# The homes of the tiles that TensorE reads: all at multiples of 512 bytes of a partition

## The chip, the cores and the metric

The kernel runs on one core of a Trainium2 chip. Its time is the device time of one execution in microseconds (us), the median of several runs. Engines are called by the profile's names: PE is TensorE's matmul, PEld its weight load, DVE is VectorE, ACT is ScalarE, POOL is GpSimd, SP is SyncE, which issues most DMAs. A tile's home is the byte of each SBUF partition at which it begins.

## What is computed

A two-layer encoder trunk on two sequences, 512 and 256 tokens, with width 1024; all in fp32:

```python
for i in range(DEPTH):                       # 2 layers
    h = rms_norm(x, norm_mix[i])
    if i % N_MIXERS == 0:                    # layer 0: attention in a window of +-128
        x = x + window_attention(h, ...)
    else:                                    # layer 1: gated depthwise convolution of width 3
        x = x + short_conv(h, ...)
    h = rms_norm(x, norm_mlp[i])
    x = x + jnp.square(jax.nn.relu(h @ mlp_w_up[i])) @ mlp_w_down[i]     # 1024 -> 4096 -> 1024
    gate = jax.nn.sigmoid(rms_norm(x, norm_ple[i]) @ ple_w_gate[i])
    x = x + (p[i] @ ple_w_proj[i]) * gate
return rms_norm(x, final_norm)
```

## The kernel before

The 768 tokens of both sequences lie along the free dimension, the 1024 features in eight blocks of 128 partitions. A product is a set of matmuls of 128 x 128 weights with 512, 384 or 256 moving columns (`H` = 384 is half of the tokens).

fp32 precision comes from three fp32r matmuls: weights and activations are each split in a high part (ScalarE copies it to fp32r) and a low part (VectorE subtracts), and high x high, high x low and low x high are added in PSUM. Weights arrive by DMA in `wraw` and are split to `whi` and `wlo`, to `zhi` and `zlo`, or to `vhi` and `vlo`. The MLPs and the convolution use a fast scheme for 2 x 2 blocks with seven products (`product7`, L498 in the profile's rows); it needs sums of weight blocks, in the tiles `sum`, and sums of activation blocks, the `t` tiles. `group` (L145) and `group2` (L135) are the plain products. Each matmul loads its own weights. The full-precision fp32 matmuls of the last norm are at L1884.

The order of the instructions on ScalarE, TensorE and VectorE is written out by hand (`manual_schedule`); semaphore waits follow from the tiles. That order and those waits are not touched by the change.

SBUF is handed out in pools, each pool's tiles one behind the other in the order in which a tag is first asked for. Tiles begin at multiples of 32 bytes. The pools that matter here:

- `const`: `vec` (gains of the norms), `sink`, `ident`, `ones32`, `ones`, `eps`.
- `slots`: the slots S0 to S31 of 768 fp32 columns (3072 bytes), in which nearly all activations live (`xs`, `t`, `act`, `aos`, `ys`, `gw`). A few tiles there have 769 columns, which the allocator rounds up to 3104 bytes (S8, S9).
- `wp`: `whi`, `wlo` (two each) and `wraw` (three), 4096 bytes each.
- `attn` and `tmpA`: what the attention stage needs, among it `ph`, `pl` and `vv` (its probabilities and values) and `L`.
- `more` and `tmpB`: take the same room after the attention stage: `zhi`, `zlo`, `vhi`, `vlo`, `sum`, slots S32 to S41 (S40 and S41 with 769 columns) and temporaries.

The small tiles of `const` shift all that stands behind them, so that few homes are at multiples of 512.

```python
def slot(i, name, dt=F32R, n=T):
    return (slots if i < 32 else more).tile([P, n], dt, tag=f"S{i}", name=name)
```

Of the kernel before, what the change touches and what calls it, by code (L numbers as in the profile page):

```python
# [11 lines left out]
F32 = mybir.dt.float32  # L12
# [6 lines left out]
P = 128  # L19
# [3 lines left out]
T = sum(SEQS)  # L23
# [5 lines left out]
CH = 1024  # L29
# [19 lines left out]
def trunk_kernel(ctx: ExitStack, tc: tile.TileContext, a: dict, out: bass.AP):  # L49
# [3 lines left out]
    const = ctx.enter_context(tc.tile_pool(name="const", bufs=1))  # L53
    main = ctx.enter_context(tc.tile_pool(name="main", bufs=1))
    slots = ctx.enter_context(tc.tile_pool(name="slots", bufs=1))
    wp = ctx.enter_context(tc.tile_pool(name="wp", bufs=2))
# [4 lines left out]
    act.preload_act_table_set(EXP_LN)  # L61
    tmp, turn, shift = None, 0, 2


    vec = const.tile([P, 7 * KB + 3 * KB], F32, name="vec")
    def gain(i, m):
# [6 lines left out]
    ident = const.tile([P, P], F32, name="ident")  # L73
# [4 lines left out]
    ones32 = const.tile([P, P], F32, name="ones32")  # L78
    dve.memset(ones32[:], 1.0)
    ones = const.tile([P, P], F32R, name="ones")  # L80
    dve.tensor_copy(ones[:], ones32[:])
    eps = const.tile([P, 1], F32, name="eps")
    dve.memset(eps[:], EPS)


    def split(hi, lo, src):
# [60 lines left out]
    more = None  # L147

    def slot(i, name, dt=F32R, n=T):

        return (slots if i < 32 else more).tile([P, n], dt, tag=f"S{i}", name=name)
# [20 lines left out]
    class Norm:  # L172


        n = T
# [327 lines left out]
    def mixer_attention():  # L503
        s1, s2 = ExitStack(), ExitStack()
        psum = s2.enter_context(tc.tile_pool(name="psK", bufs=3, space=PSUM))
        nonlocal tmp
        ap = s1.enter_context(tc.tile_pool(name="attn", bufs=2))
        tmp = s1.enter_context(tc.tile_pool(name="tmpA", bufs=3))


# [45 lines left out]
        with tc.manual_schedule(engines=order):  # L556
# [34 lines left out]
            for k in range(2):  # L591
                ph, pl = slot(10 + k, "p0h"), slot(12 + k, "p0l")
# [26 lines left out]
        with s1:  # L619
# [54 lines left out]
            vv = ap.tile([P, T // P, KV, 2, HD], F32R, name="vv", bufs=1)  # L674
# [202 lines left out]
        return xa, aos  # L877

    xa, aos = mixer_attention()
    psum = ctx.enter_context(tc.tile_pool(name="ps", bufs=8, space=PSUM))  # L880
    more = ctx.enter_context(tc.tile_pool(name="more", bufs=1))
    tmp = ctx.enter_context(tc.tile_pool(name="tmpB", bufs=1))
    pairs = [main.tile([P, 2, T], F32, tag=f"x{j}", name="x") for j in range(KB // 2)]

    def x(m, o=0, n=T):
# [1337 lines left out]
```

## Time and profile before

| | |
|---|---|
| time, median of 3 runs | 1649.18 us (1648.55 to 1649.38) |
| the profiled execution: its span, first to last instruction | 1647.0 us |
| PE busy | 1630.8 us, 9375 matmuls |
| PEld busy | 1576.5 us |
| DVE busy | 1406.5 us |
| ACT busy | 979.6 us |
| DMA | 166.35 MB, mean 101 GB/s |

For the profiled execution the page gives the span alone; the median of the runs stands 2.2 us above it. The profile's matmuls are pipelined: one starts while the one before it is still draining, so that PE's busy time says when PE had work and not how fast it ran. How fast it ran is read from the starts: the time of a stretch without a gap, divided by its matmuls. A row's "mean ns of one" holds this interval and a tail that does not depend on the shape.

### The profile page before, as it was taken

What the parts mean: (1) busy time and instruction counts of PE and PEld (TensorE: products, weight loads), DVE (VectorE), ACT (ScalarE), POOL (GpSimd) and SP (SyncE); (2) the same over time, 40 slices, a digit from 0 to 9 for tenths busy, and PEclk for the clock granted to TensorE, in tenths of its full rate; (3) what the DMA queues carried; (4) which work ended last, traced back from release to release, by engine and by line L of the source; (5) the groups of instructions that cost most, each with busy time, mean ns of one, the idle gap of its engine ahead of it and who ended that gap; (6) DMA issues with size and microseconds to landing.
All of it is one profiled execution on the core that took longest, in us unless ns stands there. A gap on an engine that the chain in (4) does not pass through costs nothing.

```text
span 1647.0 us, 24367 instructions
## 1 busy us (share of the span) xinstructions
PE 1630.8 (99%) x9375; PEld 1576.5 (96%) x9375; DVE 1406.5 (85%) x2289; ACT 979.6 (59%) x1566; POOL 82.5 (5%) x116
## 2 busy tenths in 40 slices
PE   9999999999999999999999999999999999999997
PEld 7988889999999999999999999999999999999986
DVE  7599898899889889889888777778889888988996
ACT  7378766866556556557763443555555555655764
POOL 0211000000000000000000000000000000000000
PEclk9999999999999999999999999999999999999999
DMA  8754412443323333235512122112333323333332
GB/s 272 205 134 129 141 46 84 125 106 96 90 76 91 97 96 92 72 93 147 144 64 81 66 77 77 64 64 69 92 97 96 89 76 93 96 97 92 96 117 99
DMA packets 57460, 166.35 MB, mean 101 GB/s; under 512 B 7248, under 2 KB 10832, under 8 KB 57344
## 3 DMA queue, kind: packets, MB, share of 16 engines
q1 hardware_dynamic: 45440, 139.89, 26.3%
q0 software_dynamic: 11904, 24.91, 8.6%
q8 instruction: 73, 1.20, 0.3%
q14 instruction: 43, 0.35, 0.1%
HBM read 143.02 MB, written 10.48 MB: 93 GB/s over the span
## 4 chain that ended last, share of the span: by engine, by line
PE 88%; DVE 8%; ACT 3%; issue 1%; DMA 0%; DVEq 0%; SPq 0%; ACTq 0%
PE a L498 34%; PE mm L145 9%; PE b L498 8%; PE mm L135 5%; PE d L498 5%; PE c L498 5%; PE B L498 4%; PE C L498 4%; PE gate L145 2%; PE gate L1621 2%; PE gate L1596 2%; PE pt L786 1%; PE p L1115 1%; PE p L1218 1%; PE O L796 1%
## 5 line engine op out<-in xcount | busy, mean ns | idle before, releaser
L448 ACT ACTIVATE vhi<-wraw 128x512 fp32r<-128x512 f32 x71 | 44.7, 630 | 134.6 <-PE B L498 90.3
L498 PE MATMUL a<-xs,whi 128*128 128x384 f32 x624 | 121.6, 336 | 0.0
L1391 DVE TENSOR_TENSOR x<-x,a 128x384 f32<-128x384 f32 x128 | 70.3, 553 | 55.5 <-PE a L498 55.3
L498 PE MATMUL a<-t,zhi 128*128 128x384 f32 x568 | 116.2, 337 | 0.0
L498 PE MATMUL a<-t,whi 128*128 128x384 f32 x568 | 115.8, 336 | 0.0
L498 PE MATMUL a<-act,whi 128*128 128x384 f32 x512 | 110.3, 337 | 0.0
L498 PEld LDWEIGHTS a<-xs,whi 128*128 128x128 f32 x624 | 109.9, 188 | 0.2 <-DVE y L1325 0.2
L498 PE MATMUL b<-t,zhi 128*128 128x384 f32 x536 | 108.8, 336 | 0.5 <-DVE v L261 0.5
L498 PEld LDWEIGHTS a<-t,zhi 128*128 128x128 f32 x568 | 100.5, 188 | 0.4 <-DVE t L368 0.4
L498 PEld LDWEIGHTS a<-t,whi 128*128 128x128 f32 x568 | 100.4, 188 | 0.4 <-ACT d L1493 0.4
L476 DVE TENSOR_TENSOR wlo<-wraw,whi 128x1024 fp32r<-128x1024 f32 x74 | 90.1, 1218 | 8.0 <-ACT whi L448 8.0
L498 PEld LDWEIGHTS b<-t,zhi 128*128 128x128 f32 x536 | 94.7, 188 | 0.8 <-DVE v L261 0.8
L476 DVE TENSOR_TENSOR wlo<-sum,whi 128x1024 fp32r<-128x1024 f32 x71 | 86.7, 1221 | 6.7 <-ACT whi L448 6.7
L498 PEld LDWEIGHTS a<-act,whi 128*128 128x128 f32 x512 | 91.3, 188 | 0.0
L448 ACT ACTIVATE whi<-sum 128x1024 fp32r<-128x1024 f32 x71 | 74.8, 1053 | 27.1 <-PE a L498 22.7
L448 ACT ACTIVATE whi<-wraw 128x1024 fp32r<-128x1024 f32 x76 | 79.9, 1051 | 7.0 <-PE C L498 7.0
L476 DVE TENSOR_TENSOR zlo<-sum,zhi 128x1024 fp32r<-128x1024 f32 x69 | 84.0, 1217 | 0.0
L448 ACT ACTIVATE zhi<-sum 128x1024 fp32r<-128x1024 f32 x71 | 75.1, 1058 | 12.1 <-DVE sum L424 11.2
L145 PE MATMUL mm<-xs_mix,whi 128*128 128x512 f32 (+1 forms) x320 | 81.0, 341 | 0.0
L1081 ACT ACTIVATE y<-y 128x768 f32<-128x768 f32 x62 | 52.0, 839 | 44.7 <-DVE y L1078 44.7
L362 ACT ACTIVATE t<-y 128x768 fp32r<-128x768 f32 x64 | 52.5, 840 | 43.4 <-DVE y L353 42.1
L498 PE MATMUL a<-xs,wlo 128*128 128x384 f32 x312 | 67.2, 337 | 0.0
(388 smaller groups left out, 4496.1 us busy)
## 6 DMA issues: line engine op xcount, KB each, us to landing
wraw<-in_up SPq DMA_DIRECT2D x64, 512.0 KB, 3.6
wraw<-in_down SPq DMA_DIRECT2D x64, 512.0 KB, 4.3
wraw<-in_w_in SPq DMA_DIRECT2D x24, 512.0 KB, 3.4
vlo<-in_down POOLq DMA_DIRECT2D x32, 256.0 KB, 5.8
wraw<-in_gate SPq DMA_DIRECT2D x16, 512.0 KB, 4.2
vlo<-in_up POOLq DMA_DIRECT2D x28, 256.0 KB, 5.6
pj<-pjs SPq DMA_DIRECT2D x16, 384.0 KB, 2.9
wraw<-in_w_q SPq DMA_DIRECT2D x8, 512.0 KB, 4.7
```

What stands on the lines that cost most here:

```text
L135: pe.matmul(t, lhsT=w, rhs=x[:, o:e], start=first and i == 0 and j == 0, stop=last and i == n - 1 and j == 2)
L145: pe.matmul(ps[:, o:e], lhsT=w, rhs=x[:, o:e], start=n == 0, stop=n == len(order) - 1)
L362: act.activation(t[0][:], (self.q1, self.q2)[i][:], AF.Copy)
L448: act.activation(hi[:], src, AF.Copy)
L476: dve.tensor_tensor(lo[:], src, hi[:].bitcast(F32), ALU.subtract)
L498: pe.matmul(ps, lhsT=a, rhs=b, start=start and i == 0, stop=i == len(terms) - 1, skip_group_check=True)
L786: pe.transpose(pt[:, h * P : (h + 1) * P], lg[h // 2][:, h % 2, b * P : (b + 1) * P], ident[:],)
L796: pe.matmul(O[:], lhsT=v, rhs=ph[:], start=b == 0, stop=False)
L1081: act.activation(t[:], t[:], AF.Square)
L1391: dve.tensor_tensor(t[:, o : o + H], t[:, o : o + H], f, op)
L1596: pe.matmul(t, lhsT=w[wi][k], rhs=norm.xs[part][k][:, o:e], start=k == order[0] and wi == part == 0, stop=k == order[-1] and wi == 1,)
L1621: pe.matmul(t, lhsT=wt, rhs=xt[:, b:e], start=i == j == 0 and xt is xh, stop=i == len(ts) - 1 and j == 1,)
```

## The change

The change asks for tiles earlier and in another order, so that they get other homes, and never uses what it asked for in that place: `homes` takes a tile of a tag from its pool, which fixes the tag's home, and the later code gets the same tag at that home. Fillers ("before", 96 columns, and so on) push the first of them to a multiple of 512. Tiles of odd size (`vec`, `sink`, `eps`, the 769-column slots, the bias and statistics tiles of attention) come last in their pools.

```diff
+    WIDE = 8, 9, 40, 41
+
+    def homes(pool, *tags):
+        for tag, n, *bufs in tags:
+            bufs = bufs[0] if bufs else 1
+            for _ in range(bufs):
+                pool.tile([P, n], F32, tag=tag, name="home", bufs=bufs)
+
+    def slot_homes(pool, some):
+        homes(pool, *[(f"S{i}", T) for wide in (False, True) for i in some if (i in WIDE) == wide])
+
+    homes(const, ("before", 96), ("ident", P), ("ones32", P), ("ones", P))
+    slot_homes(slots, range(32))
+    homes(wp, ("before", 112), ("whi", CH, 2), ("wlo", CH, 2))
...
     dve.memset(eps[:], EPS)
+    homes(const, ("behind", 20))
...
         ap = s1.enter_context(tc.tile_pool(name="attn", bufs=2))
+        homes(ap, ("ph", 512, 2), ("pl", 512, 2), ("vv", 4 * T))
...
     more = ctx.enter_context(tc.tile_pool(name="more", bufs=1))
+    homes(more, ("zhi", CH), ("zlo", CH), ("vhi", 512), ("vlo", 512), ("sum0", CH), ("sum1", CH))
+    slot_homes(more, range(32, 42))
     tmp = ctx.enter_context(tc.tile_pool(name="tmpB", bufs=1))
+    homes(tmp, ("before", 112))
```

In the built program no instruction is new, none is gone and none has moved, and every semaphore wait is the same. Only addresses differ. Where the tiles begin, in bytes past a multiple of 512:

| tiles | before | after |
|---|---|---|
| `whi`, `wlo`, `wraw`, `zhi`, `zlo` | 96 | 0 |
| `vhi`, `vlo`, `sum` | 160 | 0 |
| `t`, `xs`, `act`, `gw` (slots) | 32 or 96, some 64 or 128 | 0, a few (S9 and S41) 32 |
| `aos`, `ys` (slots) | 32, two `ys` 96 | 0 |
| `ph`, `pl` / `vv` | 448 / 192 | 0 / 0 |
| `ones`, `ones32`, `ident` | 0 | 0 |
| `L` (attention) | 160 | 64 |

The slices that matmuls take of these tiles begin at multiples of 512 bytes from the home. Counted over the 9126 fp32r matmuls by the bytes past a multiple of 512 at which the moving operand and the weights begin: before, 5239 have 32 and 96, 2135 have 96 and 96, 660 have 32 and 160, 330 have 32 and 32, and none has 0 and 0. After, 8674 have 0 and 0, and 436 have 32 and 0.

## The prediction

> **What bounds the kernel now.** I read the page's totals first, then the chain of work that ended last, then the busy time by stage, and last the single groups of matmuls, because only the speed of single instructions can answer to a change of addresses.
>
> ```profile
> span 1647.0 us, 24367 instructions
> PE 1630.8 (99%) x9375; PEld 1576.5 (96%) x9375; DVE 1406.5 (85%) x2289; ACT 979.6 (59%) x1566; POOL 82.5 (5%) x116
> PE 88%; DVE 8%; ACT 3%; issue 1%; DMA 0%; DVEq 0%; SPq 0%; ACTq 0%
> ```
>
> TensorE (PE) is busy nearly all the time and makes 88% of the chain; VectorE (DVE) makes 8%, ScalarE 3%, and no DMA is on it. The span, 1647.0 us, stands 2.2 us below the median of the three runs, 1649.18 us. I work out the change in the span and take it off the median.
>
> The stages differ. The columns are the stretch, its length, and busy time with instruction counts for PE, PEld (weight loads), DVE, ACT and POOL; then the granted clock and DMA. The four rows are the attention stage, the first MLP, the second MLP and the end.
>
> ```profile
> 90.00:270.00 180.00, 178.44 (x1060) 151.43 (x1059) 161.53 (x475) 130.31 (x333) 8.76 (x16) 1.00 0.38 112
> 340.00:790.00 450.00, 449.41 (x2565) 447.75 (x2564) 397.73 (x564) 269.83 (x394) 29.29 (x33) 1.00 0.35 95
> 1120.00:1570.00 450.00, 449.76 (x2564) 447.76 (x2563) 397.99 (x567) 265.17 (x392) 27.53 (x31) 1.00 0.34 94
> 1570.00:1647.00 77.00, 66.33 (x379) 57.13 (x378) 60.29 (x104) 41.86 (x72) 0.00 (x0) 0.95 0.28 94
> ```
>
> In the two MLP stages PE has no idle time worth naming: 899.2 us hold 5129 matmuls, 175.3 ns from one to the next, at a granted clock of 1.00. Only a shorter interval between matmuls shortens them. Nearly all have 384 moving columns.
>
> Is 175.3 ns fixed for that shape? These are long uninterrupted stretches of PE from the chain in order of time (start, length, engine, tile, line, count):
>
> ```profile
> 264.89 24.97 PE mm L135 x144
> 792.34 30.70 PE gate L1621 x176
> 1026.48 63.52 PE mm L135 x363
> 1107.43 16.71 PE p L1218 x96
> ```
>
> Divided by their counts they give 173.4, 174.4, 175.0 and 174.1 ns, all for 384 columns. So the interval depends a little, about 1%, on which tiles are read. Groups by shape show the same: "mean ns of one" is the interval plus a constant tail of some 162 ns (two rows further down: starts 0.23 us apart, 0.39 us long).
>
> ```profile
> L498 PE MATMUL a<-t,zhi 128*128 128x384 f32 x568 | 116.2, 337 | 0.0
> L498 PE MATMUL d<-t,vhi 128*128 128x384 f32 x328 | 64.9, 338 | 0.0
> L498 PE MATMUL b<-t,zhi 128*128 128x384 f32 x536 | 108.8, 336 | 0.5 <-DVE v L261 0.5
> L498 PE MATMUL B<-t,vhi 128*128 128x384 f32 x240 | 51.9, 338 | 0.0
> L1218 PE MATMUL p<-xs,wlo 128*128 128x384 f32 x24 | 8.1, 335 | 0.0
> L145 PE MATMUL mm<-xs_mix,whi 128*128 128x512 f32 x160 | 56.9, 400 | 0.0
> L145 PE MATMUL mm<-xs_mix,whi 128*128 128x256 f32 x160 | 34.4, 283 | 0.0
> L145 PE MATMUL gate<-xs_ple,gw 128*128 128x512 f32 x108 | 26.0, 393 | 0.0
> ```
>
> For 384 columns the means lie between 335 and 338 ns. 512 columns take 393 to 400, 256 take 283, so 128 columns more cost about 58 ns.
>
> **The change part by part.** No instruction is added, removed or moved; the fillers issue nothing. On every engine the same operations stand in the same order with the same semaphore waits, DMA issues on SP's and POOL's queues included. What changes is where tiles begin in a partition. Of 9126 fp32r matmuls (7488 of 384 columns, 898 of 256, 740 of 512), none reads both operands from a multiple of 512 bytes before; 8674 do so after. So I cost the address alone, engine by engine.
>
> DVE, ScalarE and DMA: nothing. DVE runs the same operation on tiles with different homes (wraw 96 bytes past a multiple of 512, sum 160 past):
>
> ```profile
> L476 DVE TENSOR_TENSOR wlo<-wraw,whi 128x1024 fp32r<-128x1024 f32 x74 | 90.1, 1218 | 8.0 <-ACT whi L448 8.0
> L476 DVE TENSOR_TENSOR wlo<-sum,whi 128x1024 fp32r<-128x1024 f32 x71 | 86.7, 1221 | 6.7 <-ACT whi L448 6.7
> SPq L94 <- DVE wlo L476: 426.2, 47, 14.2
> ```
>
> 1218 and 1221 ns: no dependence to speak of. The third row says that SP's queue, which fetches weights, waits for a buffer (426.2 us over 47 times), so a transfer that lands a little earlier or later stays covered by that slack. If weights were late instead, ScalarE's split and then PE would wait; the chain has 0% DMA.
>
> Weight loads: nothing by themselves. The constant tile `ones` already begins at a multiple of 512, and its loads take what the others take:
>
> ```profile
> L242 PEld LDWEIGHTS ss<-ah,ones x13: 187/188/192, 33.0 to 1616.1; 128*128 128x128 f32 x13
> L498 PEld LDWEIGHTS a<-xs,whi x624: 186/188/189, 332.1 to 1533.9; 128*128 128x128 f32 x156
> ```
>
> The median is 188 ns at home 0 and at home 96.
>
> Moving operand and weights together: this is the unknown price. Bound above (no help, some harm): all 384-column matmuls like the worst group, 338 against a mean of about 336.6, +1.4 ns x 7488 = +10.5 us; with 1 to 2 ns more on the other 1638, +13 us. Bound below: a stream of 384 columns touches four pieces of 512 bytes from an odd home (one that is no multiple of 512), three from a multiple of 512. If the whole loss of the stream came from entering a piece, each would cost 58 ns less what 128 columns take without loss. The nearest row for that is the full-precision fp32 pass at the end, whose moving tiles have odd homes too:
>
> ```profile
> 1633.82 0.59 PE L1884 MATMUL ss<-acc_final,ones 128*128 128x256 f32 x2
> 1634.25 0.68 PE L1884 MATMUL ss<-sq,ones 128*128 128x256 f32 x2
> ```
>
> Two passes of 256 columns take 0.43 us, 0.84 ns a column; if such a pass takes two steps a column, a step is 0.42 ns and 128 columns are 54 ns. One piece less then saves some 4.4 ns, x 9126 = 40 us: the lower end.
>
> Which value between? The nearest rows are the only ones where both operands begin at multiples of 64 bytes and both are read one after the other: O from pl and ph (448 past a multiple of 512) and vv (192 past).
>
> ```profile
> 172.98 0.39 PE L797 MATMUL O<-pl,vv 128*128 128x512 f32 x1
> 173.21 0.40 PE L796 MATMUL O<-ph,vv 128*128 128x512 f32 x1
> 173.44 0.28 PE L145 MATMUL mm<-xs_mix,whi 128*128 128x256 f32 x1
> 18.57 0.87 PE L145 MATMUL mm<-p0h,wlo 128*128 128x512 f32 x4
> 19.28 0.87 PE L145 MATMUL mm<-p0h,whi 128*128 128x512 f32 x4
> ```
>
> O takes 0.23 us from start to start; the neighbours from odd homes, a run of 512 and 256 columns in turn (18.57 to 19.28, four of them with another run behind), average 0.71/4 = 0.178 against (0.23+0.118)/2 = 0.174 if their long ones were like O. That is 1 to 2% in favour of homes at multiples of 64. The best long stretch, 173.4 ns, is 1.1% below the MLPs. I take that value for every 384-column matmul.
>
> Sum: the MLP stages, 5129 x (175.3 - 173.4) = 9.7 us. The other 2360 or so matmuls of 384 columns stand at about 174.6, so 1.2 ns each, 2.8 us. The 512-column ones: 393 instead of 400 would be 7 ns, but half are near 393 already and half of the rest lie in attention beside DVE and ScalarE, so I count 1.5 us. The 256-column ones: 0. Together 14 us. About 1.5 us come back where PE now arrives earlier at the copies out of PSUM and the DVE results it waits for in attention and at the end, which are not shorter. That leaves 12.5 us: 1649.2 - 12.5 = 1636.7, taken as 1637.
>
> What is late next: DVE, busy 397.7 of the 450 us of an MLP stage. At 173.4 ns PE needs 445 us, so DVE still has 47 us to spare.
>
> **Rivals.** No change: the interval is the stream's own and address patterns only shuffle it. For it: the variation is 1% although homes range over 32, 64, 96, 128, 160 and 448 past a multiple of 512; `ones` with its home at 0 is no faster, and its neighbouring starts below are 0.23 and 0.12 us apart as elsewhere. Price 0: 1649, at most 3 us off.
>
> ```profile
> 33.95 0.39 PE L242 MATMUL ss<-al,ones 128*128 128x512 f32 x1
> 34.18 0.28 PE L242 MATMUL ss<-ah,ones 128*128 128x256 f32 x1
> 34.30 0.28 PE L242 MATMUL ss<-al,ones 128*128 128x256 f32 x1
> ```
>
> [...]
>
> Slower: TensorE reads two streams at a time, the moving tile and the next weights, and after the change both always start at the same place within 512 bytes. If equal places collide, every matmul becomes like the slowest group. For it: d and B from t and v, whose usual homes, 32 and 160, are equal within 128 bytes, are the slowest at 338, b from t and z, with 32 and 96, is at 336, and the quickest stretch, L135's, has 32 and 96 throughout. Against it: in L1621's stretch two thirds of the matmuls have 96 and 96, the same place, and at 174.4 ns it beats the MLPs; and in the O rows both homes are equal within 256 bytes. Price: +10.5 to +13 us, 1660. It decides once the mean interval passes 175.1 ns, 0.4 above today's.
>
> Much faster: the odd home spoils the whole stream, and from a multiple of 512 it runs at 0.42 ns a column. Then 384 columns take 161 ns: 13.7 x 7488 = 103 us, with the other shapes (4.5 x 898, 18 x 740) 120 us, less some 15 us because PE would need 5129 x 161 = 826 us where DVE needs 796 us in the MLPs. About 1545. Against it: moving tiles with homes at 64 and 128 show none of it. [...]
>
> **How the numbers follow.** A measurement of this kernel can tell 0.2%, 3.3 us, from no change. Chances: small gain 0.40 (1609 to 1646, with 0.02 of it within 0.2%); no change 0.30; slower by collisions 0.22 (up to 1662, with 0.01 within 0.2%); much faster 0.08. Faster is 0.38 + 0.08 = 0.46, the same 0.33, slower 0.21. The range, 1609 to 1662, goes from the lower to the upper bound; it leaves out the much faster case and some 0.03 besides. The small gain's own range is 1609 to 1646.
>
> **What would show it.** Right: in the MLP stages 5129 matmuls in about 889 us instead of 899, group means at 334 to 335 ns instead of 335 to 338 with the difference between v, z and w gone, DVE's durations unchanged, and no new wait on PE. Wrong towards none: the same 175 ns a matmul. Wrong towards slower: all groups at 338 or more. Wrong towards much faster: means near 323 ns and DVE as releaser of PE in the MLPs. The step most likely to fail is the choice of 173.4 ns, since no row before reads both operands from a multiple of 512.

## The result and the profile after

| kernel | median | runs | lowest to highest |
|---|---|---|---|
| before | 1649.28 us | 4 | 1648.55 to 1650.25 us |
| changed | 1640.87 us | 4 | 1640.82 to 1641.08 us |

The ratio is 0.9948, with a 95% interval of 0.9934 to 0.9962: 8.4 us or 0.52% faster, well clear of the 0.2% that a measurement can tell. The forecast was 1637 us, a gain of 12.5.

The page's totals and the shares of the chain that ended last, changed kernel:

```profile
span 1639.3 us, 24367 instructions
PE 1623.4 (99%) x9375; PEld 1570.2 (96%) x9375; DVE 1405.6 (86%) x2289; ACT 979.7 (60%) x1566; POOL 82.5 (5%) x116
PE 90%; DVE 5%; issue 2%; ACT 2%; DMA 1%; SPq 0%; DVEq 0%; ACTq 0%; POOLq 0%
```

The span fell by 7.7 us and PE's busy time by 7.4; DVE, ScalarE and GpSimd kept theirs to 0.9 us. So the gain is in PE's own speed. The next rows show the same two MLP stretches of time (PE, PEld, DVE, ACT, POOL, each with its count, then the granted clock and DMA), and after them the long uninterrupted stretches of the chain.

```profile
340.00:790.00 450.00, 449.68 (x2586) 448.35 (x2585) 399.43 (x567) 272.99 (x398) 29.29 (x33) 1.00 0.35 95
1120.00:1570.00 450.00, 449.64 (x2568) 446.38 (x2567) 403.01 (x573) 268.75 (x396) 27.52 (x31) 1.00 0.34 94
```

```profile
264.50 24.96 PE mm L152 x144
788.98 30.57 PE gate L1642 x176
1022.09 63.44 PE mm L152 x363
1102.87 16.65 PE p L1239 x96
```

PE was as fully busy as before, at the same clock, but got through 5154 matmuls in the two stretches where it had managed 5129: 174.5 ns from one to the next instead of 175.3. The four long stretches divide to 173.3, 173.7, 174.8 and 173.4 ns; before they were 173.4, 174.4, 175.0 and 174.1. (L152 is the old L135, L1642 the old L1621, L1239 the old L1218, L515 the old L498.) The groups by shape:

```profile
L515 PE MATMUL a<-t,zhi 128*128 128x384 f32 x568 | 115.5, 335 | 0.0
L515 PE MATMUL d<-t,vhi 128*128 128x384 f32 x328 | 63.8, 334 | 0.0
L515 PE MATMUL b<-t,zhi 128*128 128x384 f32 x536 | 108.6, 335 | 0.5 <-DVE v L278 0.5
L515 PE MATMUL B<-t,vhi 128*128 128x384 f32 x240 | 51.4, 335 | 0.0
L1239 PE MATMUL p<-xs,wlo 128*128 128x384 f32 x24 | 8.0, 335 | 0.0
L162 PE MATMUL mm<-xs_mix,whi 128*128 128x512 f32 x160 | 56.8, 399 | 0.0
L162 PE MATMUL mm<-xs_mix,whi 128*128 128x256 f32 x160 | 34.8, 284 | 0.0
L162 PE MATMUL gate<-xs_ple,gw 128*128 128x512 f32 x108 | 25.5, 390 | 0.0
```

The groups of 384 columns shown here now stand at 334 or 335 ns. Of all groups of that size, d gained most, from 64.9 to 63.8 us. Of the other shapes, 512 columns gained a little, and the 256-column row grew from 34.4 to 34.8 us.

To see this without the mixing of shapes, I took the starts of all matmuls from both traces, joined them one to one, and averaged the step (the time from one start to the next) from each fp32r matmul to the next of its own size, the longer gaps left out:

| columns | pairs | before | changed | over these pairs |
|---|---|---|---|---|
| 384 | 7416 | 174.63 ns | 173.66 ns | 0.97 x 7416 = 7.2 us less |
| 512 | 449 | 232.0 ns | 229.5 ns | 2.5 x 449 = 1.1 us less |
| 256 | 656 | 117.8 ns | 119.5 ns | 1.7 x 656 = 1.1 us more |

Together 7.2 us less, nearly all of the 7.7 by which the span fell. All other steps, from one size to another and across gaps, come to 0.3 us less. The scatter of the 384-column steps fell too, from a standard deviation of 2.85 ns to 1.48.

### The profile page after: what moved, and what is told of

The parts are those of the page before. It is cut to its first block, busy times and chain, and to the rows that moved or that the text cites. A ratio compares the mean times of both kernels' runs of the same rounds, so it can differ in the third digit from the quotient of the medians.

```text
span 1639.3 us, 24367 instructions
## 1 busy us (share of the span) xinstructions
PE 1623.4 (99%) x9375; PEld 1570.2 (96%) x9375; DVE 1405.6 (86%) x2289; ACT 979.7 (60%) x1566; POOL 82.5 (5%) x116
## 4 chain that ended last, share of the span: by engine, by line
PE 90%; DVE 5%; issue 2%; ACT 2%; DMA 1%; SPq 0%; DVEq 0%; ACTq 0%; POOLq 0%
PE a L515 35%; PE mm L162 9%; PE b L515 8%; PE mm L152 5%; PE d L515 5%; PE c L515 5%; PE B L515 4%; PE C L515 4%; PE gate L162 2%; PE gate L1642 2%; PE gate L1617 2%; PE p L1239 2%; PE pt L804 1%; PE p L1136 1%; PE O L814 1%
## 5 line engine op out<-in xcount | busy, mean ns | idle before, releaser
L515 PE MATMUL a<-xs,whi 128*128 128x384 f32 x624 | 120.8, 334 | 0.0
L515 PE MATMUL a<-t,zhi 128*128 128x384 f32 x568 | 115.5, 335 | 0.0
L515 PE MATMUL a<-t,whi 128*128 128x384 f32 x568 | 115.4, 335 | 0.0
L515 PE MATMUL a<-act,whi 128*128 128x384 f32 x512 | 109.6, 335 | 0.0
L515 PEld LDWEIGHTS a<-xs,whi 128*128 128x128 f32 x624 | 109.3, 188 | 0.0
L515 PE MATMUL b<-t,zhi 128*128 128x384 f32 x536 | 108.6, 335 | 0.5 <-DVE v L278 0.5
L515 PEld LDWEIGHTS a<-t,zhi 128*128 128x128 f32 x568 | 100.1, 188 | 0.4 <-DVE t L385 0.4
L515 PEld LDWEIGHTS a<-t,whi 128*128 128x128 f32 x568 | 99.9, 188 | 0.4 <-ACT d L1514 0.4
L493 DVE TENSOR_TENSOR wlo<-wraw,whi 128x1024 fp32r<-128x1024 f32 x74 | 90.1, 1218 | 8.4 <-ACT whi L465 8.4
L515 PEld LDWEIGHTS b<-t,zhi 128*128 128x128 f32 x536 | 94.5, 188 | 0.8 <-DVE v L278 0.8
L493 DVE TENSOR_TENSOR wlo<-sum,whi 128x1024 fp32r<-128x1024 f32 x71 | 86.7, 1221 | 6.7 <-ACT whi L465 6.7
L515 PEld LDWEIGHTS a<-act,whi 128*128 128x128 f32 x512 | 90.7, 188 | 0.0
L515 PE MATMUL a<-xs,wlo 128*128 128x384 f32 x312 | 66.8, 335 | 0.0
```

Source lines behind the costliest of these rows:

```text
L493: dve.tensor_tensor(lo[:], src, hi[:].bitcast(F32), ALU.subtract)
L515: pe.matmul(ps, lhsT=a, rhs=b, start=start and i == 0, stop=i == len(terms) - 1, skip_group_check=True)
```

## The experiments

Each experiment on the kernel keeps the changed kernel's instructions, order and waits, and differs only in fillers, that is in homes. Every ratio is to the kernel before on the same chip.

**Is it the 512-byte grid, or only that homes are equal?** Two kernels give nearly all the tiles one home, but off the grid: 64 bytes past it, and 32 past it.

```diff
-    homes(const, ("behind", 20))
+    homes(const, ("behind", 40))      # all homes 64 past; 32 here for all homes 32 past
...
-    homes(tmp, ("before", 112))
+    homes(tmp, ("before", 96))        # 104 for all homes 32 past
```

> The changed kernel with every home 64 bytes further on: tiles that TensorE reads begin 64 past a multiple of 512. If a coarse grid of 512 bytes is what helps, the gain goes: about 1649 us, 175 ns a matmul in the MLP stages. If 64 bytes is the grain, it stays: 1641 us, 174.1 ns. If only the new order of the slots (which tile lies near which) helps, it stays too: 1641.

> Every home 32 bytes past a multiple of 512: moving tile and weights at equal places, as after the change, but off any grid of 64. If equal places collide off a grid of 64 (before, the weights v at 160 with t at 32 were slowest, 338 ns in the groups against 335), all groups go to 337 to 339 and the time to 1652 to 1660 us. If a grid of 512 is what counts, about 1649. If only the order of the slots counts, 1641.

Measured: 1641.45 us at 64, ratio 0.9958 [0.9944, 0.9971], and 1641.40 us at 32, ratio 0.9955 [0.9942, 0.9967]. Both have the changed kernel's speed. The groups with all homes 32 past read like the changed kernel's:

```profile
L515 PE MATMUL a<-t,zhi 128*128 128x384 f32 x568 | 115.5, 335 | 0.0
L515 PE MATMUL d<-t,vhi 128*128 128x384 f32 x328 | 63.8, 334 | 0.0
```

The multiple of 512 in the change's description does nothing by itself: nearly all homes at 0, 32 or 64 past it gave 1640.87, 1641.40 and 1641.45 us.

**Is it the homes at all, or the new order of slots?** The changed kernel's order, with fillers that put nearly all tiles back at the homes of before: slots at 32, weights at 96, v and the sums at 160. (Not quite all: 5747 matmuls have 32 and 96 and 1619 have 96 and 96, where before it was 5239 and 2135.)

```diff
-    homes(wp, ("before", 112), ("whi", CH, 2), ("wlo", CH, 2))
+    homes(wp, ("whi", CH, 2), ("wlo", CH, 2))
...
-    homes(const, ("behind", 20))
+    homes(const, ("behind", 32))
...
-    homes(more, ("zhi", CH), ("zlo", CH), ("vhi", 512), ("vlo", 512), ("sum0", CH), ("sum1", CH))
+    homes(more, ("zhi", CH), ("zlo", CH), ("fill_v", 16), ("vhi", 512), ("vlo", 512),
+          ("sum0", CH), ("sum1", CH), ("fill_s", 112))
...
-    homes(tmp, ("before", 112))
+    homes(tmp, ("before", 88))
```

> The order of the slots as after the change, but the homes of before: slots S0 to S31 at 32, S32 to S41 and the weights w and z at 96, v and sum at 160. If the homes within 512 bytes are the cause, the gain goes: 1648 to 1650 us, d and B from v at 338 again. If the order of the slots is the cause: 1641.

Measured: 1647.93 us, ratio 0.9994 [0.9986, 1.0003]: the time of before. Group d is back at its old place:

```profile
L515 PE MATMUL d<-t,vhi 128*128 128x384 f32 x328 | 64.7, 338 | 0.0
```

The order of the slots is worth nothing that can be measured; the homes carry the gain.

**The price of each pair of homes.** A kernel of matmuls alone, with the same operands over and over: 96 matmuls for each pair of a moving home and a weights home. `mo` and `wo` are the two homes. Names: n is the size (T 384, H 256, Q 512 columns), m the moving home and w the weights home, in letters O 0, A 32, B 64, C 96, D 128, E 160, F 256. (Constants are put in.)

```diff
+    for i in range(96):
+        j, k = i % 8, i // 2 % 8
+        nc.tensor.matmul(ps[:, :n], lhsT=ws[:, wo + 128 * k : wo + 128 * k + 128],
+                         rhs=xs[:, mo + 768 * j : mo + 768 * j + n], start=i == 0, stop=i == 95)
```

> Leaves the encoder out: 65 rows of 96 matmuls each, nothing else, moving homes and weight homes 0, 32, 64, 96, 128, 160, 256 past a multiple of 512 in all pairs (384 columns), eight pairs for 256 and 512 columns. Equal places off a grid of 64 collide: 32/32, 96/96, 32/160, 96/160 at 175.5 to 177 ns from start to start, 32/96 at 174, every pair with both on the grid of 64 at 173.5. A grid of 512: 0/0 alone quick, the others 174 to 176. Only the weights' home counts: each column of pairs alike whatever the moving home.

Measured, with the moving tile at 32 and the weights at 32, 64, 96, 128 and 160 (differences 0, 32, 64, 96, 128):

```profile
L41 PE MATMUL nTmAwA<-xs,ws 128*128 128x384 f32 x96 | 16.8, 334 | 0.0
L41 PE MATMUL nTmAwB<-xs,ws 128*128 128x384 f32 x96 | 16.8, 336 | 0.0
L41 PE MATMUL nTmAwC<-xs,ws 128*128 128x384 f32 x96 | 16.9, 336 | 0.0
L41 PE MATMUL nTmAwD<-xs,ws 128*128 128x384 f32 x96 | 17.1, 340 | 0.0
L41 PE MATMUL nTmAwE<-xs,ws 128*128 128x384 f32 x96 | 17.1, 338 | 0.0
```

From the starts these are 173.6, 173.3, 174.7, 176.6 and 176.0 ns. The rows teach a caution: at a difference of 32 the mean of one reads 336, as many groups of the slower kernel did, though its matmuls follow each other as quickly as at 334. The mean of one is not the interval plus a constant, as I had taken it to be. For a row without gaps the busy time is the better reading.

Pairs at 0 and 0 (173.3 in a later sweep), 64 and 64 or 128 and 128 (16.8 us and 334 ns in both rows) are as quick as 32 and 32. None of the three expectations came true. In these rows it counts not where the two homes are, but how far apart: weights 128 on read 17.1 us and 338 ns with the moving tile at 0, at 32 and at 128.

**Does the kernel follow?** Four kernels keep the moving tiles together and move weights, z, v and the sums away by one difference; some 7970 of the 9126 fp32r matmuls then have it. Here is 128, with the filler sizes of the others in comments (for 64 on, the filler of `tmp` changes as well, to 104):

```diff
-    homes(wp, ("before", 112), ("whi", CH, 2), ("wlo", CH, 2))
+    homes(wp, ("before", 16), ("whi", CH, 2), ("wlo", CH, 2))   # 120 for 32 on, 32 for 192 on, none for 64 on
...
-    homes(const, ("behind", 20))
+    homes(const, ("behind", 24))                                # 32 for 64 on (slots at 32, weights at 96)
...
-    homes(more, ..., ("sum0", CH), ("sum1", CH))
+    homes(more, ..., ("sum0", CH), ("sum1", CH), ("fill_s", 96))   # 120 for 32 on, 80 for 192 on, 112 for 64 on
```

> The changed kernel with TensorE's moving tiles at 0 and its weights w, z, v (and attention's ph, pl, vv) at 128 past a multiple of 512, one difference nearly everywhere. If the difference between the two homes sets the interval, the sweep's 176.0 ns against 173.6 holds: +2.4 x 7488 = +18 us on 1641, with the other shapes +1 to +3: 1657 to 1662 us, slower than before. If only a mixture of differences is bad and any uniform one is good: 1641. If multiples of 64 or 128 for every home are what helps: 1641.

> Moving tiles at 32, all weights at 96 past a multiple of 512: the commonest pair of before, made uniform. By the difference: the sweep's 174.66 against 173.6 ns, +1.05 x 7488 = +8 us on 1641, other shapes about 0: 1647 to 1651 us, as before. If a mixture is what hurts: 1641.

> Moving tiles at 0, weights at 32. By the difference: the sweep has 173.33 against 173.6 ns for 384 columns (-2 us) but 233 against 227 for 512 columns (+4 us) and 118.3 against 119.8 for 256 (-1 us): 1640 to 1643 us. If homes off a grid of 64 bytes hurt where the two are not equal: 1648 or more.

> Moving tiles at 0, weights w, z, v at 192. The full sweep has 173.3 ns at a difference of 192 as at 0, and 176 at 128: by the difference 1640 to 1643 us (384 columns as at 0; 512 columns 228.9 against 226.7, 256 columns 117.8 against 120.0). If any difference but 0 and 32 costs in the whole kernel, or the further apart the worse: 1649 to 1658.

| weights on by | median | ratio, 95% interval | 384-column step in the kernel | in the sweeps |
|---|---|---|---|---|
| 0 (changed kernel) | 1640.87 us | 0.9948 [0.9934, 0.9962] | 173.66 ns | 173.3 ns |
| 32 | 1641.35 us | 0.9955 [0.9942, 0.9969] | 173.65 ns | 173.3 ns |
| 64 | 1648.98 us | 0.9999 [0.9990, 1.0008] | 174.82 ns | 174.6 ns |
| 128 | 1655.81 us | 1.0043 [1.0031, 1.0056] | 175.87 ns | 176.0 ns |
| 192 | 1640.14 us | 0.9948 [0.9934, 0.9961] | 173.52 ns | 173.3 ns |

The kernel follows the sweeps. With 64 everywhere, which most of the kernel before had, all the gain is gone. With 128 it is slower than before; I had expected 1657 to 1662 and missed by 1.2 us, since I counted 2.4 ns for each 384-column matmul where the step rose by 2.2, and the steps across gaps took 2 us less. At 128 past, at 64 past and at 192 past, the same two groups:

```profile
L515 PE MATMUL a<-t,zhi 128*128 128x384 f32 x568 | 116.9, 338 | 0.0
L515 PE MATMUL d<-t,vhi 128*128 128x384 f32 x328 | 64.6, 338 | 0.0
```

```profile
L515 PE MATMUL a<-t,zhi 128*128 128x384 f32 x568 | 116.5, 337 | 0.0
L515 PE MATMUL d<-t,vhi 128*128 128x384 f32 x328 | 64.1, 336 | 0.0
```

```profile
L515 PE MATMUL a<-t,zhi 128*128 128x384 f32 x568 | 115.6, 336 | 0.0
L515 PE MATMUL d<-t,vhi 128*128 128x384 f32 x328 | 63.9, 336 | 0.0
```

One of the three has the time of before, one is some 15 us slower than the changed kernel, and the last is as quick as it with means that still say 336.

**One part alone.** Only v and the sums 128 on, all else at 0:

```diff
-    homes(const, ("behind", 20))
+    homes(const, ("behind", 24))
...
-    homes(more, ("zhi", CH), ("zlo", CH), ("vhi", 512), ...
+    homes(more, ("zhi", CH), ("zlo", CH), ("fill_v", 32), ("vhi", 512), ..., ("fill_s", 96))
```

> The changed kernel with v and sum alone 128 bytes further on, as far from t as before. By the difference only the 852 matmuls of d and B that read v get slower, 2.4 to 2.7 ns each, 2.0 to 2.3 us: 1643 us, their groups at 338 and all others at 334 to 335. If the mixture of differences slows its neighbours too: 1645 to 1648.

Measured: 1642.67 us, ratio 0.9965 [0.9953, 0.9978], 1.8 us above the changed kernel's median. Only the groups that read v paid:

```profile
L515 PE MATMUL a<-t,zhi 128*128 128x384 f32 x568 | 115.5, 335 | 0.0
L515 PE MATMUL d<-t,vhi 128*128 128x384 f32 x328 | 64.8, 338 | 0.0
L515 PE MATMUL B<-t,vhi 128*128 128x384 f32 x240 | 51.9, 337 | 0.0
```

These are nearly the 64.9 and 51.9 us that d and B had before, where v's homes were 128 from t's.

**The whole map, and bf16.** The sweep again with 16 by 16 homes, 48 matmuls each, letters A 0, B 32 and so on to P 480; then rows with mixed homes, and rows of bf16 tiles.

```diff
-HOMES = {"O": 0, "A": 32, "B": 64, "C": 96, "D": 128, "E": 160, "F": 256}
+HOMES = {c: 32 * i for i, c in enumerate("ABCDEFGHIJKLMNOP")}
```

> Leaves the encoder out: rows of 48 matmuls of 384 columns alone, all 256 pairs of homes that are multiples of 32 within 512 bytes; rows whose moving tile alternates between two homes; five rows in bf16. If the difference sets the interval: every diagonal (weights' home minus moving home, the same) is alike: 0 at 173.3 to 173.6, +32 at 173.3, +64 at 174.7, +96 to +160 at 176 to 176.7. If absolute homes count, rows or columns of the table stand out instead. An alternating row (32 and 96 with weights at 96) lies at 174 to 175.5 as in the kernel before, above both 173.6 and the mean with 174.7 if the change of phase itself costs. bf16 reads half the bytes for each column: if the loss belongs to reads at 4 bytes a column, its intervals are shorter and alike for differences of 0, 64 and 128; if it belongs to the array, they are as long as fp32r's.

Measured, the moving tile at 256 (I) and the weights at 256 to 480 (I to P); columns are start, length, engine, line, names and count. Divide the difference of two starts by 48:

```profile
1171.62 8.51 PE L47 MATMUL mIwI<-xs,ws 128*128 128x384 f32 x48
1179.96 8.49 PE L47 MATMUL mIwJ<-xs,ws 128*128 128x384 f32 x48
1188.28 8.55 PE L47 MATMUL mIwK<-xs,ws 128*128 128x384 f32 x48
1196.67 8.64 PE L47 MATMUL mIwL<-xs,ws 128*128 128x384 f32 x48
1205.15 8.61 PE L47 MATMUL mIwM<-xs,ws 128*128 128x384 f32 x48
1213.60 8.64 PE L47 MATMUL mIwN<-xs,ws 128*128 128x384 f32 x48
1222.08 8.48 PE L47 MATMUL mIwO<-xs,ws 128*128 128x384 f32 x48
1230.40 8.64 PE L47 MATMUL mIwP<-xs,ws 128*128 128x384 f32 x48
1238.88 8.48 PE L47 MATMUL mJwA<-xs,ws 128*128 128x384 f32 x48
```

For example 8.32/48 = 173.3 ns at J (32 on), 8.48/48 = 176.7 at L (96 on), and 8.32/48 = 173.3 again at O (192 on). At I the 8.34 us give 173.8, because the row's first three steps take 185, 175 and 182 ns before it settles. Within rows, from the ninth matmul on:

| weights' home less moving home, modulo 256 bytes | 0 | 32 | 64 | 96 | 128 | 160 | 192 | 224 |
|---|---|---|---|---|---|---|---|---|
| ns from start to start, 384 columns | 173.3 | 173.3 | 174.6 | 176.6 | 176.0 | 176.6 | 173.3 | 176.6 |

The table holds for 248 of the 256 pairs wherever the two homes stand. The other 8 all lie in the first two weights' homes after a change of the moving home, and they keep another value to the end of their row: with the moving home at 192 and the weights at 0, a difference of 64, it is 176.6 ns. So what ran before a pair counts as well as its difference. Of mixed rows, moving homes 32, 32, 96, 96 in turn with weights at 96 take 175.0 ns, though half of the pairs are equal. The kernel before mixed the two in the same way. With the addresses of the built program joined to its trace, its pairs of 96 and 96 took 175.4 ns from start to start and those of 32 and 96 took 174.0, the other way round from the table. The equal pairs there came in short runs: the second step of such a run took 179.5 ns on average, and from the sixth on it was 173.3. The bf16 rows, differences of 0, 64 and 128 (the last row closes the third):

```profile
2255.67 7.97 PE L47 MATMUL bfmAwA<-xb,wb 128*128 128x384 bf16 x48
2263.48 7.96 PE L47 MATMUL bfmAwC<-xb,wb 128*128 128x384 bf16 x48
2271.28 7.96 PE L47 MATMUL bfmAwE<-xb,wb 128*128 128x384 bf16 x48
2279.08 7.96 PE L47 MATMUL bfmBwD<-xb,wb 128*128 128x384 bf16 x48
```

7.80/48 = 162.5 ns each: these three differences do not matter to bf16; the others were not tried. The fp32r rows of 384 columns are up to 3.3 ns apart by nothing but the two homes (173.3 to 176.6 ns), and none came below 173.2.

**Is it the length of the weight load?** If loads took turns with the moving stream, loading fewer weight columns would shorten the step. Matmuls alone once more, the moving tile at 0, with 128 (W), 96 (X), 64 (Y) or 32 (Z) weight columns and 256 (H), 384 (T) or 512 (Q) moving columns; the rows below are at equal homes (a):

```diff
-                lhsT=ws[:, wo + 128 * k : wo + 128 * k + 128],
+                lhsT=ws[:, w // 4 + 128 * k : w // 4 + 128 * k + cols],
```

> Leaves the encoder out: rows of 64 matmuls with 256, 384 or 512 moving columns from home 0 and weights of 128, 96, 64 or 32 columns, the weights' home 0 to 224 bytes on. In the first sweep equal homes took 119.8, 173.3 and 227 ns for 256, 384 and 512 columns, 13 ns over 106.7, 160 and 213.3 each, a constant. If that constant is the weight load taking turns from the moving stream, half the weights halve it: 64 columns of weights give 166.7 ns at 384, 32 columns give 163 to 164, and with 64 columns the difference between homes shrinks too. If it is a cost of each matmul, all widths stay at 173.3. A difference at which 384 columns take 173.3 and 256 or 512 take less than at 0 would make a better kernel than the changed one.

```profile
L40 PE MATMUL cWnTda<-xs,ws 128*128 128x384 f32 x64 | 11.3, 335 | 0.0
L40 PE MATMUL cZnTda<-xs,ws 128*32 128x384 f32 x64 | 11.3, 336 | 0.0
L40 PE MATMUL cYnTda<-xs,ws 128*64 128x384 f32 x64 | 11.3, 336 | 0.0
L40 PE MATMUL cWnHda<-xs,ws 128*128 128x256 f32 x64 | 7.8, 283 | 0.0
L40 PE MATMUL cZnHda<-xs,ws 128*32 128x256 f32 x64 | 7.4, 276 | 0.0
L40 PE MATMUL cWnQda<-xs,ws 128*128 128x512 f32 x64 | 14.7, 390 | 0.0
L40 PE MATMUL cZnQda<-xs,ws 128*32 128x512 f32 x64 | 15.0, 394 | 0.0
```

At equal homes a quarter of the load leaves the step of 384 columns at 173.3 ns. So at this size the 11 ns that fp32r takes over bf16 (173.3 against 162.5) are not the time of the loads. The other sizes do not follow: from 128 to 32 weight columns the step of 256 columns falls from 119.8 to 113.3 ns, and that of 512 rises from 227.2 to 231.4. So loads that simply take turns with the moving stream do not explain the rows, but neither does a cost that each matmul has whatever its load. (With 96 weight columns, 384 take 174.9 ns at equal homes and 173.5 at a difference of 128, which fits neither.) At 384 columns a difference of 128 costs 0.2 ns at most with 64 or 32 weight columns and 2.7 ns with 128; a difference of 64 costs 1.2 to 1.5 ns with all three. The load does take part in the loss that the homes cause, but I cannot say how. No difference in this run gave a step at 384 columns clearly below 173.3 ns. The 106.7, 160 and 213.3 ns of the expectation are, within 0.3 ns, 53.4 ns for each 128 columns, by which the first sweep's rows at equal homes differ (119.9, 173.3 and 226.7 ns).

## Why the prediction was right, and where it was not

- **The cost sits in the address alone: right.** The streams are the same, DVE's splits took what they took (1218 and 1221 ns), and the kernel with the old homes has the old time.

```profile
L493 DVE TENSOR_TENSOR wlo<-wraw,whi 128x1024 fp32r<-128x1024 f32 x74 | 90.1, 1218 | 8.4 <-ACT whi L465 8.4
L493 DVE TENSOR_TENSOR wlo<-sum,whi 128x1024 fp32r<-128x1024 f32 x71 | 86.7, 1221 | 6.7 <-ACT whi L465 6.7
```

- **No new wait on PE: nearly.** One is new, once, for a weights transfer (us in all, times, longest):

```profile
PE p L1239 <- DMA wlo<-in_up: 0.6, 1, 0.6
```

  It makes the chain turn off into that transfer, 19.14 us of issue and 7.51 us of DMA, and so the shares of the chain changed (issue 2%, DMA 1%) though PE lost only 0.6 us.
- **173.4 ns for every 384-column matmul: the term that was mis-sized.** Forecast 9.7 + 2.8 = 12.5 us; measured 7.2 over the pairs. The step came down to 173.66 on average and not to 173.4. By the addresses, steps between equal pairs do reach 173.4 from the sixth of a run on; the first steps of runs, and the 402 matmuls of this size that still read a tile 32 past (S9 and S41), make up the rest. Worse, I set 173.4 against 175.3, which is the MLP stretch divided by its matmuls and holds the odd longer gap and the other sizes; from a 384-column matmul to the next it was 174.63. The saving per matmul was 0.97 ns, not 1.2 to 1.9.
- **512 columns, 1.5 us: about right** (1.1 over the pairs). **256 columns, 0: wrong.** They lost 1.1 us. In the first sweep 256 columns take 119.9 ns at equal homes and 113.5 at a difference of 64, the other way round from 384 (173.3 and 174.7) and 512 (226.7 and 233.4). The change trades one for the other, and the kernel has more of the long ones. The last sweep has 117.8 for 256 columns at a difference of 64, so at this size the difference alone does not set the step.
- **1.5 us given back at the waits for copies: not seen.** The steps outside the three rows of the table, the waits among them, got 0.3 us shorter.
- **The reason for the gain: wrong.** I argued from homes off a grid of 64 or 512, and put the loss down to pieces of 512 bytes. Equal homes off the grid are as quick (1641.40 and 1641.45 us). The evidence that I leaned on, the O pair with homes 448 and 192, has a difference of 256 bytes: by the map that is an equal pair. I had noted that fact and used it only against a rival.
- **The rival "slower": backwards.** The loads do overlap the matmuls (PEld 1570.2 us and PE 1623.4 us busy in a span of 1639.3), but equal places do not slow the matmuls; at 384 columns they are the quick ones, 173.3 ns in the sweeps. I came to it from v at 160 with t at 32, "equal within 128 bytes". By the map the period is 256, and a difference of 128 is one of the slow ones, 176.0 ns. **"No change"** would have come true with another filler: weights 64 on give 1648.98 us. **"Much faster"** had no run for it: no fp32r row of 384 columns reached 161 ns, the lowest stands at 173.2. Its 0.42 ns a column is close to the 0.417 a column by which the first sweep's rows grow, but no run shows that a full-precision pass takes two steps a column.

So the right direction was partly luck: the row from which I took it, O's, was an equal pair by the map too. The 173.4 ns was luck as well. I took it from the stretch of L135, all at a difference of 64, and it happens to be close to what equal homes give.

**Still open.** The mechanism inside the chip; no trace shows it. Why that stretch of L135 ran at 173.4 ns where the sweep has 174.6 (with weights 64 on it does so again: 24.97 us for 144). Why a difference of 96 took 173.3 ns in the last sweep and 176.6 nearly everywhere in the other two. The eight exceptions of the map and the slow first steps of a run show that the order of the steps matters beside the homes; by what rule was not tried.

## What to carry to other kernels

In a PE-bound fp32r kernel, look at the home of the moving tile and of the weights together: what counted here is their difference modulo 256 bytes, and 0 was a good choice for 384 and 512 columns (173.3 and 226.7 ns), while 128 was a bad one for 384 (176.0 ns). In the kernel before, equal pairs that stood in short runs among others gained nothing (175.4 ns on average); they came to 173.3 ns only from the sixth of a run on. It was worth 0.5% here, and 0.9% between differences of 0 and 128, so only after all else, and fillers that made all homes equal were enough; no grid was needed (1641.40 us off it, 1640.87 on it). To read such effects, take steps from start to start between equal shapes, since a stretch divided by its count (175.3 ns before, where the steps gave 174.63), or the mean of one, mixes in other things.

## What the runs showed that I had not expected

- An fp32r step of 384 columns depends on the difference of two homes modulo 256 bytes, up to 1.9% (173.3 to 176.6 ns), and on what ran before it; a bf16 step did not at the three differences tried (162.5 ns).
- At equal homes the fp32r steps of the first sweep were about 119.9, 173.3 and 226.7 ns for 256, 384 and 512 columns: 53.4 ns for each 128 columns, so 0.417 ns a column (an estimate from these rows) and 13 ns that do not grow with the columns, as a cost per piece of 512 bytes would.
- Fewer weight columns, 32 instead of 128, do not shorten the step of 384 columns at equal homes; that of 256 columns they shorten by 6.5 ns, and that of 512 they lengthen by 4.2.
